# The triangular inverses of a gated delta rule: 128x128 products against 32x32 squares on the diagonal of the array, with background tasks held to one step in two ticks

## The chip, the cores and the metric

The kernel runs on one core of a Trainium2 chip. The metric is the device time of one execution in microseconds; the number to beat is the median of several runs. TensorE (PE) multiplies, VectorE (DVE) and ScalarE (ACT) do the elementwise work, GpSimd (POOL) sets up masks, and SyncE (SP) issues the transfers. Each engine works its own instructions strictly in the order in which the program hands them over, and waits where an operand is not there yet.

## The reference

A trunk of two layers on 256 tokens of width 2048, each a token mixer and an MLP of width 8192. The mixer of layer 0 is what the change touches: eight heads of a gated delta rule and eight heads of band attention behind one input projection, joined by one output projection. Per head and chunk of 64 tokens the delta rule needs the inverse of a unit lower triangular matrix:

```
lower = jnp.where(strict, jnp.einsum('bhnid,bhnjd->bhnij', kb, kc) * decay, 0.0)
tmat  = triangular_solve(eye + lower, eye)          # 64 x 64, unit lower triangular
u = tmat @ (vc * beta);   w = tmat @ (kb * exp(gcum))
# scan over the chunks:
v_new = u_n - w_n @ state
o_n   = qd_n @ state + qk_n @ v_new
state = state * gl_n + kd_n.T @ v_new
o = rms_norm(o, norm_w) * silu(z)
```

The kernel takes chunks of 128 tokens instead of 64, so its triangular matrices are 128x128, and there are two of them per head (t = 0, 1).

## The kernel before

**The big stream.** All large products are streamed: 1 MB of weights arrives in a `raw` buffer (4 of them), ACT rounds it to `wh`, DVE forms the rest `wl = raw - wh`, and PE multiplies both with activations that are split the same way. One such megabyte is an *item*. An item hands over its matmuls in four pieces, and after each piece the program makes a *tick*. At a tick the scheduler `tick` may step the task at the head of the `fast` list (evacuations of projections), steps `bg_n` background tasks (`bg_step`, round robin over `self.bg`), and pumps the modulation job: 1 MB rows (`mraw`) that DVE multiplies and sums (L466). So the order of the side work against the big stream is set by ticks, and each engine's queue is the result. Big products into `pg` belong to the input projections, those into `pw` to the output projections and later parts.

**The first mixer.** After the partial sums of the projections come, in this order, eight last parts, then blocks of four items each: attention v, two gate projections in a small item, attention q, k, v of the second head group, and `GZ`, `GZ + 1`, the gates z of delta-rule groups 0 and 1. Then the output projection `out_blocks` starts; its first two items take the units of group 0 (`o[0]`) and of attention group 0 (`o[2]`), the third takes `o[3]` and `o[1]`, and `o[1]` is delta-rule group 1. Where a unit is asked for and isn't finished, `unit_of` and `gdn_z` step its task to the end on the spot.

**The delta rule.** The background tasks are two groups of four heads (`gdn_group`; group 1 starts when group 0 is done, `gdn_after`) and two attention groups. A group runs `gdn_tile` for t = 0, 1 in lockstep: norms, decay E, values V, the matrix `lt` (transposed lower part, 128x128 for each head), `Pt` for the output. Then comes the inverse by doubling, s = 2, 4, 8, 16, 32, 64: with X the inverse of the diagonal blocks of size s, `y = mask(lt.T x)`, `x = x - xt.T y`, then `xt` is x transposed by PE and copied by ACT. Each level is 4 + 4 products of 128x128 in f32 and 4 transposes, for each t. Only the blocks on the diagonal hold anything, but the products run over the whole 128x128. Then the tail of the group, one chain: `gvn` = Xt V, `gS` = kd v, `gR`, `gvn` of t = 1, the outputs `go` through `Pt`, squares, a root by Newton's steps (`gor`, `goss`, `goy`, `gon`, `got`), the scaling, transposes into the result. `gdn_z` multiplies with the gate and splits for the output projection.

`bg_n` is 1.5 here: one and a half background steps at each tick.

Of the kernel before, what the change touches and what calls it, by code (L numbers as in the profile page):

```python
# [12 lines left out]
I32 = mybir.dt.int32  # L13
AF = mybir.ActivationFunctionType
# [4 lines left out]
P = 128  # L19
# [20 lines left out]
class Task:  # L40


    def __init__(self, gen):
        self.gen, self.done, self.result = gen, False, None
        self.n, self.frees = 0, 10000
# [67 lines left out]
class Trunk:  # L113
# [8 lines left out]
    def __init__(self, tc, ctx, ins, out):  # L122
# [15 lines left out]
        self.ticks = 0  # L138
# [74 lines left out]
    def bg_step(self):  # L213
        for _ in range(len(self.bg)):
            t = self.bg.pop(0)
            ok = t.step()
            if not t.done:
                self.bg.append(t)
            if ok:
                return True  # L220
# [190 lines left out]
    def masks(self):  # L411
# [16 lines left out]

        self.M = {}
        for s in (2, 4, 8, 16, 32, 64):  # L430
            nb = P // (2 * s)
            m = self.const([P, nb, s], f"lev{s}")
            g.memset(m, 1.0)
            g.affine_select(out=m, in_=m, compare_op=ALU.is_ge, fill=0.0, base=-s, pattern=[[-2 * s, nb], [0, s]], channel_multiplier=1)
            g.affine_select(out=m, in_=m, compare_op=ALU.is_ge, fill=0.0, base=2 * s - 1, pattern=[[2 * s, nb], [0, s]], channel_multiplier=-1)
            self.M[s] = m

        self.M1T = self.const([P, 64, 2], "lev1T")
        g.memset(self.M1T, 0.0)
        v = self.M1T[:, :, 1:2]  # L440
        g.memset(v, 1.0)
        g.affine_select(out=v, in_=v, compare_op=ALU.is_equal, fill=0.0, base=0, pattern=[[-2, 64], [0, 1]], channel_multiplier=1)
        self.M1T = self.M1T.rearrange("p b c -> p (b c)")
# [613 lines left out]
    def gdn_tile(self, hg, t, kf, qf, vf, G):  # L1057
# [54 lines left out]

        xt = self.s2(tag="gXt")
        nc.vector.tensor_tensor(xt, lt, self.row(self.M1T), op=ALU.mult)
        nc.vector.tensor_tensor(xt, self.row(self.ident), xt, op=ALU.subtract)
# [8 lines left out]
        ps = self.pm()  # L1124
        for h in range(4):
            self.tr(ps[:, h], xt[:, h])
        x = self.s2(tag="gX")
        nc.scalar.copy(x, ps)
        G["X" + str(t)] = x
        yield  # L1130


        for s in (2, 4, 8, 16, 32, 64):
            nb = P // (2 * s)
            part = lambda a, n: a.rearrange("p h (b n c) -> p h b n c", n=2, c=s)[:, :, :, n]
            ps = self.pm()
            for h in range(4):
                self.mm(ps[:, h], lt[:, h], x[:, h])
            y = self.s2(tag="gY")
            nc.gpsimd.memset(y, 0.0)  # L1140
            nc.vector.tensor_tensor(part(y, 0), part(ps, 0), self.M[s].unsqueeze(1).to_broadcast([P, 4, nb, s]), op=ALU.mult)
            yield
# [696 lines left out]
```

## Time and profile before

| | |
|---|---|
| median of 3 runs | 2692.22 us (2691.31 to 2695.09) |
| the profiled execution | 2696.17 us, its span 2694.1 us |
| mean granted TensorE clock | 0.993 |
| busy: PE, DVE, ACT, POOL | 98%, 80%, 50%, 1% of the span |
| last copy of group 1's result (L1238) | starts at 448.9 us |
| second item of the output projection | starts at 489.1 us |

PE and its weight loads (PEld) are listed apart. A row of a group gives line, engine, operation, out<-in by the program's names, shape and count, then busy time and the mean of one. In f32 each product is two records of PE, so 192 records of `gX,gLt` are 96 products. A record's time includes the way through the array; the distance from one record to the next is shorter, and it is that distance which adds up. A row of the timeline gives start, length, engine, line, operation, count, and in square brackets the idle time before it with what ended it.

### The profile page before, as it was taken

Reading aid. Unit: us, or ns where it says so; the run is one execution under the profiler, and the core shown is the slowest. Engines: PE = TensorE matmul, PEld = TensorE weight load, DVE = VectorE, ACT = ScalarE, POOL = GpSimd, SP = SyncE. Lnnn points to the kernel's source line nnn. Section 1 sums busy time; section 2 is a strip of 40 time slices with the busy share of each in tenths; the row PEclk is TensorE's granted clock in tenths of the full one; section 3 lists DMA queues with packets and bytes.
Section 4 is the critical chain, followed back from the end, with each engine's and each line's share of the span. In section 5 each row is a group of like instructions: output and inputs, shape, how many; then the busy total and the mean of one; then the engine's idle time right before and its main releaser. Section 6 shows DMA issues by size and latency. Waiting matters only on the chain.

```text
span 2694.1 us, 40013 instructions
## 1 busy us (share of the span) xinstructions
PE 2636.1 (98%) x15834; PEld 2324.7 (86%) x15834; DVE 2153.1 (80%) x3106; ACT 1347.7 (50%) x1990; POOL 24.2 (1%) x98
## 2 busy tenths in 40 slices
PE   5999999999999999999999999999999999999999
PEld 4887989888888888888888888888888888888888
DVE  7998998997888888889889876897787855555554
ACT  3445455456355354454556544665555354454452
POOL 1000000000000000000000000000000000000000
PEclk7999999999999999999999999999999999999999
DMA  9986487867899899898556665555557855555553
GB/s 351 346 327 235 173 305 273 327 239 288 313 344 327 332 330 332 334 331 307 177 190 216 230 235 203 204 188 174 201 199 286 321 194 188 188 188 188 190 194 133
DMA packets 100459, 680.08 MB, mean 252 GB/s; under 512 B 11184, under 2 KB 14512, under 8 KB 19376
## 3 DMA queue, kind: packets, MB, share of 16 engines
q1 hardware_dynamic: 95376, 669.07, 68.5%
q10 hardware_dynamic: 4896, 8.46, 1.0%
q8 instruction: 124, 2.03, 0.3%
q14 instruction: 63, 0.52, 0.1%
HBM read 675.33 MB, written 2.16 MB: 251 GB/s over the span
## 4 chain that ended last, share of the span: by engine, by line
PE 87%; DVE 7%; DMA 3%; ACT 2%; issue 1%; ACTq 0%; DVEq 0%; SPq 0%
PE pw L332 67%; PE pg L332 13%; PE pm L335 3%; PE pm L332 2%; DVE mraw L466 2%; DVE wl L346 2%; DMA mraw<-in_mod_dram 2%; PE pm L339 1%; DMA raw<-in_w_ab_dram 1%; ACT wh L342 0%; DVE u L1619 0%; DVE hf L893 0%; DVE u L896 0%; ACT pm L1075 0%; DMA sd_rowd<-sd_rows 0%
## 5 line engine op out<-in xcount | busy, mean ns | idle before, releaser
L342 ACT CAST wh<-raw 128x1024 fp32r<-128x1024 f32 x870 | 905.6, 1051 | 985.8 <-PE pw L332 697.2
L346 DVE TENSOR_TENSOR wl<-raw,wh 128x1024 fp32r<-128x1024 f32 x870 | 1053.2, 1223 | 428.3 <-ACT wh L342 426.8
L332 PE MATMUL pw<-u,wh 128*128 128x512 f32 x5584 | 1318.9, 391 | 2.9 <-DVE u L896 1.7
L332 PEld LDWEIGHTS pw<-u,wh 128*128 128x128 f32 x5584 | 1032.7, 188 | 209.9 <-issue 1.9
L332 PEld LDWEIGHTS pw<-u,wl 128*128 128x128 f32 x5584 | 702.1, 191 | 23.5 <-DVE wl L346 2.0
L332 PE MATMUL pw<-u,wl 128*128 128x256 f32 x5584 | 712.3, 283 | 2.6 <-ACT u L342 1.4
L466 DVE SCALAR_TENSOR_TENSOR mraw<-mraw,crow 128x2048 f32<-128x2048 f32 x192 | 438.9, 2288 | 20.5 <-DMA mraw<-in_mod_dram 20.3
L332 PE MATMUL pg<-wh,u 128*128 128x512 f32 x864 | 279.5, 396 | 0.0
L332 PEld LDWEIGHTS pg<-wh,u 128*128 128x128 f32 x864 | 162.0, 188 | 33.2 <-issue 0.7
L958 DVE SCALAR_TENSOR_TENSOR x<-pw,mod,x 128x256 f32<-128x256 f32 x352 | 162.0, 480 | 32.5 <-PE pw L332 29.9
L332 PE MATMUL pg<-wl,u 128*128 128x512 f32 x432 | 169.5, 392 | 0.3
L332 PE MATMUL pg<-u,wh 128*128 128x256 f32 x672 | 124.5, 285 | 0.0
L332 PEld LDWEIGHTS pg<-u,wh 128*128 128x128 f32 x672 | 105.5, 192 | 0.3
L332 PEld LDWEIGHTS pg<-wl,u 128*128 128x128 f32 x432 | 81.2, 188 | 17.9 <-DVE wl L346 1.7
L332 PE MATMUL pg<-u,wl 128*128 128x256 f32 x336 | 95.4, 284 | 0.0
L332 PE MATMUL pm<-u,wh 128*128 128x256 f32 (+1 forms) x340 | 64.0, 292 | 19.2 <-ACT wh L342 19.2
L332 PEld LDWEIGHTS pm<-u,wh 128*128 128x128 f32 x340 | 54.3, 199 | 20.3 <-ACT wh L342 20.0
L332 PEld LDWEIGHTS pg<-u,wl 128*128 128x128 f32 x336 | 64.4, 192 | 0.0
L1017 DVE SCALAR_TENSOR_TENSOR u<-pad,cst,u 128x256 f32<-128x256 f32 x144 | 60.4, 484 | 3.9 <-ACT u L1011 3.8
L1531 ACT ACTIVATE rl<-rs 128x512 f32<-128x512 f32 x64 | 40.5, 633 | 27.7 <-DVE rs L1526 25.1
L1525 ACT COPY rs<-pw 128x512 f32<-128x512 f32 x64 | 36.8, 576 | 34.5 <-PE pw L332 34.5
L895 ACT ACTIVATE u<-hf,mod 128x256 fp32r<-128x256 f32 x64 | 29.4, 502 | 49.4 <-DVE hf L893 49.4
(298 smaller groups left out, 1525.9 us busy)
## 6 DMA issues: line engine op xcount, KB each, us to landing
raw<-in_w_dram SPq DMA_DIRECT2D x256, 1024.0 KB, 5.2
mraw<-in_mod_dram SPq DMA_DIRECT2D x192, 1024.0 KB, 6.1
raw<-in_w_ab_dram SPq DMA_DIRECT2D x56, 1024.0 KB, 5.7
raw<-in_w_ssd_dram SPq DMA_DIRECT2D x48, 1024.0 KB, 4.9
raw<-in_w_sz_dram SPq DMA_DIRECT2D x32, 1024.0 KB, 4.8
raw<-in_wo_ssd_dram SPq DMA_DIRECT2D x32, 1024.0 KB, 4.9
raw<-in_wo_ab_dram SPq DMA_DIRECT2D x16, 1024.0 KB, 5.4
sE<-sd_rowd ACTq DMA_DIRECT2D x32, 256.0 KB, 4.9
```

The costliest lines, as they stand in the source:

```text
L332: return self.nc.tensor.matmul(o, a, b, start=start, stop=stop, skip_group_check=True)
L335: self.nc.tensor.matmul(o, lhsT, rhs, start=True, stop=True, skip_group_check=True)
L339: return self.nc.tensor.transpose(o, a, self.anti if flip else self.ident[:k, :k])
L342: a = self.nc.scalar.copy(hi, src)
L346: b = self.nc.vector.tensor_tensor(lo, src, hi.bitcast(F32), op=ALU.subtract)
L466: x = nc.vector.scalar_tensor_tensor(raw, raw, 1.0, self.crow, op0=ALU.mult, op1=ALU.mult, accum_out=t[:, f : f + 1])
L895: nc.scalar.activation(hi, h[:, f], AF.Identity, bias=shift[:, col])
L958: self.last = nc.vector.scalar_tensor_tensor(x[:, 2 * b + f], ps[:, f, n], g[:, 2 * cb + f : 2 * cb + f + 1], x[:, 2 * b + f], op0=ALU.mul ...
L1017: nc.vector.scalar_tensor_tensor(h, pad[:, f, 1 + q : 257 + q], w[:, q, j : j + 1], h, op0=ALU.mult, op1=ALU.add)
L1525: nc.scalar.copy(lo, ps[:, :, 1])
L1531: nc.scalar.activation(rl, lo, AF.Relu)
```

## The change

**The inverse.** `gdn_tile` ends after `Pt`; the inverse moves to a function of its own, `gdn_inverse`, that runs once per group for both t and all four heads (eight matrices). The levels s = 2 to 16 stay inside 32x32 squares on the diagonal: the four squares of a matrix lie on partitions 0, 32, 64, 96, and the product of each square is a matmul of 32 rows, 32 columns and 32 moving columns in its own corner of the array, 32 of them per product step. `x`, `xt`, `y` are 128x256 for all eight matrices together. The transposes go from PE and ACT to DVE, which transposes 32x32 squares. The 32 level is 16 + 24 such small products, and the 64 level 8 + 8 products of 64x64, written into `XT` (128x128 for each head; zeroed by POOL). The masks become 32 wide.

**The beat.** `Task` gets a time `at`, and `bg_step` passes over a task whose time has not come; a step that did something sets `at = ticks + gap`. `gap` is 2 in the first mixer and 0 elsewhere. So a background task steps at most once in two ticks, where a lone task made up to three steps in two ticks before. The flag that lets attention group 0 start (`self.prep`) is set when both tiles are through, before the inverse.

**What it does to the order.** In all excerpts pm, pg, pw are PSUM tiles, and the number behind a name is the program's running number. PE, the levels of group 1's inverse. Before, they stand between the items of attention v and of z (pg):

```order
L332 MATMUL pg_3808<-wl_4035,u_1713 128x512
L339 MATMUL pm_3712<-ident,gX_3587 128x128 x4
L335 MATMUL pm_3718<-gX_3587,gLt_3522 128x128 x4
L339 MATMUL pm_3726<-ident,gX_3594 128x128 x4
L335 MATMUL pm_3732<-gX_3594,gLt_3535 128x128 x4
L332 MATMUL pg_3808<-wh_4034,u_1713 128x512
L335 MATMUL pm_3748<-gY_3723,gXt_3527 128x128 x4
L332 MATMUL pg_3808<-wh_4034,u_1713 128x512
L332 MATMUL pg_3808<-wl_4035,u_1713 128x512
```

Now they stand between the first two items of the output projection (pw); this is the level s = 8 and the one after it, in the second of these items:

```order
L336 MATMUL pm_4808<-gX_4442,gLt_4289 32x32 x16
L336 MATMUL pm_4808<-gX_4442,gLt_4299 32x32 x16
L336 MATMUL pm_4852<-gY_4841,gXt_4441 32x32 x32
L333 MATMUL pw_5168<-u_4317,wh_4756 128x512 x4
L333 MATMUL pw_5168<-u_4318,wh_4756 128x512 x4
L336 MATMUL pm_4887<-gX_4442,gLt_4289 32x32 x16
L336 MATMUL pm_4887<-gX_4442,gLt_4299 32x32 x16
L333 MATMUL pw_5168<-u_4788,wh_4760 128x512 x4
L333 MATMUL pw_5168<-u_4789,wh_4760 128x512 x4
L333 MATMUL pw_5168<-u_4317,wl_4757 128x256
L336 MATMUL pm_4922<-gY_4920,gXt_4441 32x32 x32
```

So this part moved by some nine items down the stream. PE, the tail of group 1, before:

```order
L335 MATMUL pm_4005<-gV_3493,gXt_3527 128x128 x4
L332 MATMUL pg_4202<-u_761,wh_4194 128x256
L332 MATMUL pg_4202<-u_761,wl_4195 128x256
L332 MATMUL pg_4202<-u_761,wh_4194 128x256 x2
L332 MATMUL pg_4202<-u_761,wl_4195 128x256
L332 MATMUL pg_4202<-u_761,wh_4194 128x256 x2
L332 MATMUL pg_4202<-u_761,wl_4195 128x256
L335 MATMUL pm_4020<-gvn_4010,gkd_3316 128x128 x4
L332 MATMUL pg_4202<-u_761,wh_4194 128x256 x2
```

and now, from the 64 level on (`gX_651` is `x64`):

```order
L336 MATMUL pm_5016<-gX_651_4455,gLt_4299 64x64 x4
L336 MATMUL pm_5027<-gXT_4453,gY_5025 64x64 x4
L336 MATMUL pm_5027<-gXT_4454,gY_5025 64x64 x4
L336 MATMUL pm_5038<-gV_4226,gXT_4453 128x128 x4
L336 MATMUL pm_5045<-gvn_5043,gkd_3980 128x128 x4
L336 MATMUL pm_5052<-gS_5050,u_2425 128x128 x4
L336 MATMUL pm_5062<-gS_5050,u_2521 128x128 x4
L336 MATMUL pm_5069<-gR_5057,gXT_4454 128x128 x4
L336 MATMUL pm_5077<-gvn_5043,gPt_4347 128x128 x4
L336 MATMUL pm_5088<-gvn_5074,gPt_4354 128x128 x4
L340 MATMUL pm_5122<-ident,go_5082 128x128 x4
L340 MATMUL pm_5128<-ident,go_5093 128x128 x4
```

The big products are gone from between the links; ahead of these rows the 32 level stands likewise without them, down from the end of the second `pw` item, and the third begins behind them. DVE at the same place, before:

```order
L1180 TENSOR_TENSOR gvn_4010<-pm_4005,gbe_3415 128x512
L346 TENSOR_TENSOR wl_4264<-raw_4257,wh_4263 128x1024
L1193 SCALAR_TENSOR_TENSOR gR_4049<-pm_4044,gd_neg,gV_3500 128x128 x4
L1198 TENSOR_TENSOR gqS_4059<-pm_4054,gd_eg 128x512
L1204 TENSOR_TENSOR gvn_4074<-pm_4069,gbe_3442 128x512
L466 SCALAR_TENSOR_TENSOR mraw_4467,mod_126<-mraw_4467,crow 128x2048
L1216 TENSOR_TENSOR go_4112<-gqS_4059,pm_4107 128x512
```

and now:

```order
L478 SCALAR_TENSOR_TENSOR mraw_5310,mod_126<-mraw_5310,crow 128x2048
L1196 TENSOR_SCALAR gX_651_4455<-pm_4986 32x8x32
L486 TENSOR_TENSOR mod_126<-mod_126,cst 128x4
L1213 TENSOR_SCALAR gXT_4453<-pm_5027 64x4x64
L1213 TENSOR_SCALAR gXT_4454<-pm_5027 64x4x64
L478 SCALAR_TENSOR_TENSOR mraw_5364,mod_127<-mraw_5364,crow 128x2048
L1237 TENSOR_TENSOR gvn_5043<-pm_5038,gbe_4102 128x512
L486 TENSOR_TENSOR mod_127<-mod_127,cst 128x4
L488 SCALAR_TENSOR_TENSOR mod_127<-mod_127,cst 128x4
L1250 SCALAR_TENSOR_TENSOR gR_5057<-pm_5052,gd_neg,gV_4233 128x128 x4
L1255 TENSOR_TENSOR gqS_5067<-pm_5062,gd_eg 128x512
L1261 TENSOR_TENSOR gvn_5074<-pm_5069,gbe_4129 128x512
```

One multiplication of the modulation job (L478 there, L466 before) stands ahead of the links `gX_651` and `gvn`. SP's queue differs in one place only: two weight transfers are issued ahead of one `mraw` instead of behind it.

The diff (the masks cut short):

```diff
--- before.py
+++ after.py
@@ -42,7 +42,7 @@
 
     def __init__(self, gen):
         self.gen, self.done, self.result = gen, False, None
-        self.n, self.frees = 0, 10000
+        self.n, self.frees, self.at = 0, 10000, 0
 
     def step(self):
 
@@ -135,7 +135,7 @@
         self.fast, self.bg, self.open = [], [], []
         self.fast_n, self.bg_n = 0.5, 0.5
         self.credit = self.fcredit = 0.0
-        self.ticks = 0
+        self.ticks = self.gap = 0
         self.pending = self.early = self.etask = None
         self.pin = self.still = 0
         self.after_ins = self.gate = None
@@ -213,10 +213,11 @@
     def bg_step(self):
         for _ in range(len(self.bg)):
             t = self.bg.pop(0)
-            ok = t.step()
+            ok = t.at <= self.ticks and t.step()
             if not t.done:
                 self.bg.append(t)
             if ok:
+                t.at = self.ticks + self.gap
                 return True
         return False
 
@@ -426,21 +427,32 @@
+        def diagonal(name, full):
+
+            m = self.const([P, 32], name)
+            for b in range(4):
+                B = slice(32 * b, 32 * b + 32)
+                g.tensor_copy(m[B], full[B, B])
+            return m
+
+        self.I32 = diagonal("I32", self.ident)
         self.M = {}
-        for s in (2, 4, 8, 16, 32, 64):
+        for s in (2, 4, 8, 16):
...
+            self.M[s] = diagonal(f"lev{s}", full)
...
+        self.M1T = diagonal("lev1T", full)
@@ -1109,10 +1121,7 @@
         lt = self.s2(tag="gLt")
         for h in range(4):
             nc.vector.scalar_tensor_tensor(lt[:, h], ps[:, h], be[:, h : h + 1], E[:, h], op0=ALU.mult, op1=ALU.mult)
-
-        xt = self.s2(tag="gXt")
-        nc.vector.tensor_tensor(xt, lt, self.row(self.M1T), op=ALU.mult)
-        nc.vector.tensor_tensor(xt, self.row(self.ident), xt, op=ALU.subtract)
+        G["lt", t] = lt
         yield
         ps = self.pm()
         for h in range(4):
@@ -1121,41 +1130,89 @@
         nc.vector.tensor_tensor(p1, ps, E, op=ALU.mult)
         G["Pt", t] = p1
         yield
-        ps = self.pm()
-        for h in range(4):
-            self.tr(ps[:, h], xt[:, h])
-        x = self.s2(tag="gX")
-        nc.scalar.copy(x, ps)
-        G["X" + str(t)] = x
-        yield
-
-
-        for s in (2, 4, 8, 16, 32, 64):
-            nb = P // (2 * s)
-            part = lambda a, n: a.rearrange("p h (b n c) -> p h b n c", n=2, c=s)[:, :, :, n]
-            ps = self.pm()
-            for h in range(4):
-                self.mm(ps[:, h], lt[:, h], x[:, h])
-            y = self.s2(tag="gY")
-            nc.gpsimd.memset(y, 0.0)
-            nc.vector.tensor_tensor(part(y, 0), part(ps, 0), self.M[s].unsqueeze(1).to_broadcast([P, 4, nb, s]), op=ALU.mult)
-            yield
-            ps = self.pm()
-            if s < 64:
-                for h in range(4):
-                    self.mm(ps[:, h], xt[:, h], y[:, h])
-                nc.vector.tensor_tensor(part(x, 0), part(x, 0), part(ps, 0), op=ALU.subtract)
-                yield
-                ps = self.pm()
-                for h in range(4):
-                    self.tr(ps[:, h], x[:, h])
-                nc.scalar.copy(xt, ps)
+
+    def gdn_inverse(self, G):
+
+
+
+        nc = self.nc
+        lt = [G["lt", t] for t in range(2)]
+        heads = [(4 * t + h, t, h) for t in range(2) for h in range(4)]
+        B = [slice(32 * b, 32 * b + 32) for b in range(4)]
+        sub = [slice(4 * t, 4 * t + 4) for t in range(2)]
+        tile = lambda tag: self.s2([P, 8, 32], tag=tag)
+        flat = lambda a: a.rearrange("p n c -> p (n c)")
+        psum = lambda: self.pm([P, 512])[:, :256].rearrange("p (n c) -> p n c", c=32)
+        rep = lambda m, n: m.unsqueeze(1).to_broadcast([m.shape[0], n, 32])
+        xt, x = tile("gXt"), tile("gX")
+        for t in range(2):
+            for b in B:
+                nc.vector.tensor_tensor(xt[b, sub[t]], lt[t][b, :, b], rep(self.M1T[b], 4), op=ALU.mult)
+        nc.vector.tensor_tensor(xt, rep(self.I32, 8), xt, op=ALU.subtract)
+        nc.vector.transpose(flat(x), flat(xt))
+        XT = [self.s2(tag="gXT") for _ in range(2)]
+        x64 = self.s2([P, 8, 64], tag="gX6")
+        for z in XT:
+            nc.gpsimd.memset(z, 0.0)
+        nc.gpsimd.memset(x64[B[0], :, 32:], 0.0)
+        yield
+
+        for s in (2, 4, 8, 16):
+            ps = psum()
+            for n, t, h in heads:
+                for b in B:
+                    self.mm(ps[b, n], lt[t][b, h, b], x[b, n])
+            y = tile("gY")
+            nc.vector.tensor_tensor(y, ps, rep(self.M[s], 8), op=ALU.mult)
+            yield
+            ps = psum()
+            for n, t, h in heads:
+                for b in B:
+                    self.mm(ps[b, n], xt[b, n], y[b, n])
+            nc.vector.tensor_tensor(x, x, ps, op=ALU.subtract)
+            if s < 16:
+                nc.vector.transpose(flat(xt), flat(x))
             else:
-                for h in range(4):
-                    self.mm(ps[:, h], y[:, h], xt[:, h])
-                nc.vector.tensor_tensor(part(xt, 1), part(xt, 1), part(ps, 1), op=ALU.subtract)
-                yield
-        G["Xt", t] = xt
+                for t in range(2):
+                    for b in B:
+                        nc.vector.transpose(XT[t][b, :, b], x[b, sub[t]])
+            yield
+
+        ps = psum()
+        for n, t, h in heads:
+            for p in (0, 2):
+                self.mm(ps[B[p + 1], n], lt[t][B[p], h, B[p + 1]], x[B[p], n])
+        y = tile("gY")
+        for p in (0, 2):
+            nc.scalar.copy(y[B[p + 1]], ps[B[p + 1]])
+        nc.gpsimd.tensor_copy(x64[B[0], :, :32], x[B[0]])
+        nc.gpsimd.tensor_copy(x64[B[1], :, 32:], x[B[1]])
+        yield
+        ps = psum()
+        for n, t, h in heads:
+            self.mm(ps[B[1], n], XT[t][B[1], h, B[1]], y[B[1], n])
+            for p in (0, 2):
+                self.mm(ps[B[p], n], y[B[p + 1], n], XT[t][B[p + 1], h, B[p + 1]])
+        nc.vector.tensor_scalar(x64[B[1], :, :32], ps[B[1]], -1.0, None, op0=ALU.mult)
+        for t in range(2):
+            for p in (0, 2):
+                nc.scalar.activation(XT[t][B[p], :, B[p + 1]], ps[B[p], sub[t]], AF.Copy, scale=-1.0)
+        yield
+
+        lower, upper = slice(0, 64), slice(64, P)
+        ps = self.pm([P, 8, 64])
+        for n, t, h in heads:
+            self.mm(ps[upper, n], lt[t][lower, h, upper], x64[lower, n])
+        y = self.s2([P, 8, 64], tag="gY")
+        nc.scalar.copy(y[upper], ps[upper])
+        yield
+        ps = self.pm([P, 8, 64])
+        for n, t, h in heads:
+            self.mm(ps[lower, n], y[upper, n], XT[t][upper, h, upper])
+        for t in range(2):
+            nc.vector.tensor_scalar(XT[t][lower, :, upper], ps[lower, sub[t]], -1.0, None, op0=ALU.mult)
+            G["Xt", t] = XT[t]
+        yield
 
     def gdn_group(self, hg, kc, qc, vc, gates):
 
@@ -1169,9 +1226,9 @@
             for t in tiles:
                 if not t.done:
                     t.step()
-            if all("X" + str(n) in G for n in range(2)):
-                self.prep[hg].done = True
-            yield
+            yield
+        self.prep[hg].done = True
+        yield from self.gdn_inverse(G)
 
         ps = self.pm()
         for h in range(4):
@@ -1667,7 +1724,7 @@
                                  ((0, (2,)), (0, (3, 4)), (0, (5,)), (1, (0, 1)), (1, (2,)), (1, (3, 4)), (1, (5,))))
         self.rate, self.rate2 = 0.25, 1.1
         self.fast_n = 0.8
-        self.bg_n = 1.5
+        self.bg_n, self.gap = 1.5, 2
         o, res = [None] * 4, {}
         put = lambda key, gen: res.__setitem__(key, self.evac(gen))
         self.prep = [Flag(), Flag()]
@@ -1739,7 +1796,7 @@
                 self.c_blocks(w, (cb,), hl, lambda ps, cb: conv_sink(ps, cb, then))
 
         self.rate = 0.0
-        self.bg_n = 0.75
+        self.bg_n, self.gap = 0.75, 0
         self.fast_n = 0.5
         for half in range(2):
             G = range(half * 4, half * 4 + 4)
```

18 lines of the change are left out of this document (9 added, 9 removed).

## The prediction

> **What bounds the kernel now.** I read the page first, then busy time by stretches around the delta rule, then PE's waits there, then the timeline.
>
> ```profile
> span 2694.1 us, 40013 instructions
> PE 2636.1 (98%) x15834; PEld 2324.7 (86%) x15834; DVE 2153.1 (80%) x3106; ACT 1347.7 (50%) x1990; POOL 24.2 (1%) x98
> ```
>
> ```profile
> 260.00:340.00 80.00, 79.79 (x535) 72.09 (x534) 77.08 (x172) 37.91 (x85) 6.12 (x18) 1.00 0.49 179
> 380.00:440.00 60.00, 60.00 (x468) 56.75 (x467) 55.51 (x100) 27.37 (x63) 3.99 (x8) 1.00 0.83 305
> 465.00:560.00 95.00, 94.96 (x592) 85.55 (x591) 92.41 (x131) 49.59 (x79) 0.00 (x0) 1.00 0.89 325
> ```
>
> The columns are the stretch, its length, then PE, PEld, DVE, ACT, POOL, the granted clock and the transfers. In the first two stretches the two inverses run, in the third the output projection. PE is full in all three and DVE stands just behind it (77.08 of 80). PE's waits from 240 to 560 us come to 3.1 us, and nearly all of it is two links of chains:
>
> ```profile
> PE pm L339 <- DVE go L1230: 1.4, 2, 0.7
> PE pm L339 <- DVE aq L1283: 0.8, 1, 0.8
> ```
>
> Since a busy PE need not be at its peak, I checked by the distance between records. In the chain of work, eight f32 records of 128 columns take 0.89 us and four transposes 0.44 us, so 0.111 us each; 16 `pw` products of 512 columns start 3.70 us before what follows them, 0.231 us each.
>
> ```profile
> 281.56 0.89 PE pm L335 x8
> 282.45 0.44 PE pm L339 x4
> ```
>
> ```profile
> 489.11 3.86 PE L332 MATMUL pw<-u,wh 128*128 128x512 f32 x16
> 492.81 4.12 PE L332 MATMUL pw<-u,wl 128*128 128x256 f32 x33
> 496.76 3.59 PE L332 MATMUL pw<-u,wh 128*128 128x512 f32 x15
> ```
>
> 33 products of 256 columns take 3.95 us, 0.120 us each, so an item of 16 + 16 needs 5.6 us of PE, and products stand back to back. PE's work sets the time here: a microsecond of it saved is a microsecond gained, and a microsecond in which PE must wait with nothing to do is lost.
>
> **The change part by part: PE's work.** What goes:
>
> ```profile
> L335 PE MATMUL pm<-gX,gLt 128*128 128x128 f32 x192 | 25.2, 275 | 0.0
> L335 PE MATMUL pm<-gY,gXt 128*128 128x128 f32 x160 | 20.0, 275 | 0.0
> L339 PE MATMUL pm<-ident,gX 128*128 128x128 f32 x80 | 12.3, 273 | 0.0
> L335 PE MATMUL pm<-gXt,gY 128*128 128x128 f32 x32 | 4.1, 275 | 0.0
> L339 PE MATMUL pm<-ident,gXt 128*128 128x128 f32 x16 | 2.4, 274 | 0.0
> ```
>
> 480 records at 0.111 us are 53.3 us. What comes, per group: 4 levels of 32 + 32 products of 32 columns, 16 + 24 for the 32 level, that is 296 products or 592 records, and 16 products of 64x64. For two groups 1184 small records and 64 of 64 columns. No product of 32 columns is in the trace. The nearest is the second layer's `sx,sE`: 64 columns, two halves of the array in turn.
>
> ```profile
> 1733.74 1.11 PE L332 MATMUL pw<-u,wl 128*128 128x256 f32 x8
> 1734.79 2.09 PE L335 MATMUL pm<-sx,sE 128*64 128x64 f32 x64
> 1736.80 3.14 PE L332 MATMUL pw<-u,wl 128*128 128x256 f32 x24
> ```
>
> 64 records in 2.01 us: 0.031 us, where half of 0.111 would be 0.056; the halves overlap by a factor 1.77. For 32 columns a quarter of 0.111 is 0.028 if squares don't overlap; with the same factor it would be 0.016; and if squares pay as a 64-column record alone, 0.056. I take 0.028, since it is nearest to the one dense row of short records, 0.031. So 1184 x 0.028 = 33.2 us. The 64 records of 64x64 all lie in one quarter, so nothing overlaps: 64 x 0.056 = 3.6 us. Entering a burst: eight products at 0.120 from 1733.74 end at 1734.70, the burst starts at 1734.79, so 0.09 us; 24 bursts make 2.1. PE's work: -53.3 + 33.2 + 3.6 + 2.1 = **-14.4 us**.
>
> The Trainium skill ("TensorE: Matmul & The Clock Gate", Part 1, on the issue floor) says that starts of matmuls never come closer than about 25 ns however few columns stream. By that the 1184 records would take at least 29.6 us and the sum would be some 3.6 us lower at best; no run here shows the floor, and 0.031 does not contradict it.
>
> **DVE, ACT, POOL.** DVE loses 24 `gY` and 20 `gX` operations and what forms the first `xt`:
>
> ```profile
> L1141 DVE TENSOR_TENSOR gY<-pm,lev 128x256 f32<-128x256 f32 x24 | 9.9, 423 | 0.6 <-PE pm L335 0.6
> L1328 DVE TENSOR_SCALAR as<-as,asum 128x128 f32<-128x128 f32 x5 | 1.4, 283 | 0.0
> L1345 ACT COPY u<-pm 128x256 f32<-128x256 f32 x5 | 1.8, 368 | 7.4 <-PE pm L332 7.4
> L466 DVE SCALAR_TENSOR_TENSOR mraw<-mraw,crow 128x2048 f32<-128x2048 f32 x33 | 75.5, 2289 | 1.0 <-DMA mraw<-in_mod_dram 1.0
> ```
>
> 44 operations at 0.42 are 18.5 us. What is left per group is 9 operations and 4 transposes of 128x256 and 19 small ones of 128 to 512 elements; taking 0.42 and 0.28 to 0.35 for them (a transpose on DVE is not in the trace; from 0.28, the smaller row, to twice 0.42) that is about 11 us a group. With the forming of `xt` that goes too, DVE ends some 3 us lower; hidden behind PE either way, except in the chain below. ACT loses its 24 copies of `xt` and `x`, POOL its 24 memsets; neither bounds. The new masks on POOL (24 copies of squares) fall into the first 25 us and are first read after 260 us, so I cost them at nothing.
>
> **What the beat does to group 1.** A group is some 30 steps: 7 for the tiles, 13 for the inverse, about 10 for the tail. At one step in two ticks two groups want 120 ticks. From the start of group 0 to the output projection there are 3 last parts and 20 items of the blocks, 23 x 4 = 92 ticks. So the last 28 ticks' worth is not hidden: the levels fall beside the first two output items, 8 ticks, and what remains is stepped to the end when the third item asks for `o[1]`. That is the piece of the order without big products. In the levels the cover is 5 to 15 big products a step (0.7 to 1.9 us) against an answer of DVE of 0.42 us, behind other operations of DVE; from the order and these durations I find about 0.9 us of wait at s = 8, where two bursts follow each other, and 0.6 elsewhere: **+1.5 us**.
>
> **The bare chain.** Its second half stands in the trace of before, hidden:
>
> ```profile
> 427.27 1.13 PE L335 MATMUL pm<-gV,gXt 128*128 128x128 f32 x8
> 428.43 0.69 DVE L1180 TENSOR_TENSOR gvn<-pm,gbe 128x512 f32<-128x512 f32 x1 [0.98 <-PE pm L335]
> 429.18 1.15 PE L335 MATMUL pm<-gvn,gkd 128*128 128x128 f32 x8
> 431.01 2.05 PE L335 MATMUL pm<-gS,u 128*128 128x128 f32 x16
> 434.81 1.09 PE L335 MATMUL pm<-gvn,gPt 128*128 128x128 f32 x8
> 436.81 0.69 DVE L1216 TENSOR_TENSOR go<-gqS,pm 128x512 f32<-128x512 f32 x1
> 438.49 0.28 ACT L1218 ACTIVATE pm<-go 128x128 f32<-128x128 f32 x1
> 438.92 0.28 ACT L1218 ACTIVATE pm<-go 128x128 f32<-128x128 f32 x1
> 439.79 0.17 DVE L1224 TENSOR_TENSOR goss<-goss,gor 128x8 f32<-128x8 f32 x1 [0.37 <-ACT pm L1218]
> 439.99 0.17 DVE L1225 TENSOR_TENSOR goss<-goss,gor 128x8 f32<-128x8 f32 x1
> ```
>
> From 427.27 to the last `Pt` products' end at 435.9 it takes 8.6 us; one `mraw` (2.29) now stands ahead of `gvn`, and another ahead of `go`. I add up from the end of the s = 16 update. 32 level: products 0.9, copy of `y` by ACT 0.7 (two at up to 0.37), in their place eight transposes behind a `wl`, so 3.7 in all; 24 products 1.35; `mraw` 2.29 and the copy to `x64` 0.35, or ACT's four scalings, 1.2: to 7.0. 64 level: 0.9, 0.6 (ACT copy), 0.9, two operations 0.7, and hand-overs of 0.1 to 0.2: to 10.5. Tail to `Pt`: 8.6 and half of `mraw`, since it starts while `gV` still runs: to 20.2. `go` behind `mraw`: 22. Four squares at 0.43: 23.7. Sixteen short operations at 0.20: 26.9. Two scalings at 0.69, transposes, ACT's copies: 30. Gate and split (0.75 and 0.69 twice each, with ACT's casts): **33 us**. In it PE works on 32 + 48 short records (2.2), 32 of 64 columns (1.8), 56 of 128 (6.2) and 17 others (1.9), 12 us, all counted above. So PE stands **21 us** with nothing to do.
>
> The clock falls with it. In the second layer PE waited 2.35 us for `sE`, and:
>
> ```profile
> 1407.70 1.76 PE L335 MATMUL pm<-sx,sE 128*64 128x64 f32 x32 [2.35 <-DVE sE L1433]
> 1409.39 2.34 PE L332 MATMUL pw<-u,wh 128*128 128x512 f32 x5
> ```
>
> ```profile
> 1407.80:1408.80 1.00, 1.00 (x24) 1.00 (x26) 1.00 (x3) 0.00 (x0) 0.00 (x0) 0.60 0.96 193
> 1409.80:1410.80 1.00, 1.00 (x3) 0.75 (x3) 1.00 (x3) 0.00 (x0) 0.00 (x0) 0.50 1.07 428
> 1411.80:1412.80 1.00, 1.00 (x6) 0.84 (x5) 0.52 (x1) 0.57 (x1) 0.00 (x0) 1.00 1.02 338
> ```
>
> Granted clock 0.5 to 0.6 for some 3.6 us, and 32 records took 1.69 instead of 1.0 us. After the bare chain about 3.6 us at half speed cost 1.8, and some bursts inside run slow: **+3 us** (0 to 6). One of the waits of 3.1 us goes with the old place of the tail: **-1 us**.
>
> Sum: -14.4 + 1.5 + 21 + 3 - 1 = **+10.1 us**. The profiled execution took 2696.17 us, 4 us above the median of the runs; against the median 2692.22 I get **2702 us**.
>
> **Rivals.** *The squares overlap.* At 0.016 us (the halves' factor) PE's work falls by another 14.2 us, and with a chain that is 3 us shorter the time is 2685: faster by 0.27%. It decides from about 0.019 us a record down (there the sum is zero). For it speaks the overlap of `sx,sE`; against it that an f32 product's two records go to the same square one after the other, so only neighbours can overlap. The Trainium skill ("TensorE: Matmul & The Clock Gate", Part 3) would have different squares start about 4 ns apart, which is this rival at its strongest; its floor of Part 1 speaks against it. No run here has shown either.
>
> *The squares are dear.* At 0.056 us, if changes of shape or weight loads bar any hiding, PE's work rises by 33 us instead: 2735. Against it: the 64-column burst at 0.031 has a new weight load for each record too.
>
> *The chain is covered.* If the 33 us were 22, because ACT and DVE had nothing else queued, PE would idle 11 us less and the sum is -1: 2691, no change. Against it: the `mraw` rows in the order, and the row at 439.79.
>
> **How the numbers follow.** A time within 0.2% (5.4 us) of before can't be told from no change with runs that lie 3.8 us apart. Chances: my sum, with its 0.025 to 0.031 and a chain of 28 to 38 us, 0.57 (2695 to 2712; a fifth of it within 0.2%); overlap 0.17, two thirds of it faster by over 0.2%; covered chain 0.12, two thirds of it no change; dear squares 0.14. So faster 0.15, same 0.24, slower 0.61. The range leaves out the strongest overlap and the top of the dear squares: 2686 to 2725.
>
> **What would show it.** In the profile after: a burst of 64 small records 1.8 us long (right), 1.0 (overlap) or 3.6 (dear); PE's waits, 3.1 us before from 240 to 560, near 25 us and headed by `gvn`, `go` and `u` of group 1; a slice with a granted clock near 0.5 before the third output item. If PE's waits there stay below 10 us, the chain was covered and I am wrong on the main term.

## The result, and the profile after

The changed kernel takes 2716.4 us (median of 5 runs, 2714.2 to 2719.9) against 2694.0 of the kernel before beside it: ratio 1.0084, 95% interval 1.0073 to 1.0095. It is 22.4 us slower; 10.1 were forecast. The squares were the smaller part of the story: they turned out far cheaper than I took them, and the kernel lost all the same, because TensorE now stands idle or runs at half clock for longer than was saved.

The page of the changed kernel, and its three stretches that were shown of before:

```profile
span 2712.3 us, 41498 instructions
PE 2622.2 (97%) x16602; PEld 2299.3 (85%) x16602; DVE 2153.9 (79%) x3114; ACT 1340.3 (49%) x1980; POOL 27.9 (1%) x106
```

```profile
260.00:340.00 80.00, 70.73 (x628) 56.28 (x627) 77.74 (x176) 40.19 (x110) 2.09 (x10) 0.94 0.65 246
380.00:440.00 60.00, 57.23 (x447) 54.34 (x446) 56.63 (x120) 33.58 (x92) 1.70 (x4) 1.00 0.87 322
465.00:560.00 95.00, 76.20 (x733) 67.06 (x732) 72.30 (x130) 34.88 (x71) 1.71 (x2) 0.84 0.54 203
```

Before, PE was full in all three (79.79 of 80, 60.00 of 60, 94.96 of 95). Now it has 9 us of nothing in the first, and the granted clock falls to 0.94; DVE is as full as it was (77.74 against 77.08). In the third, where the bare chain lies, PE, DVE and the clock all fall.

All but the first six records of a burst of squares in the timeline after, with what follows them:

```profile
460.40 0.70 PE L336 MATMUL pm<-gX,gLt 32*32 32x32 f32 x58
461.04 0.94 PE L333 MATMUL pm<-aT,u 128*128 128x128 f32 x6
```

These are 58 records in 0.64 us, 0.011 us each, and 0.70 us for 64. I had set down 1.8 us for such a burst if right, 1.0 for overlap, 3.6 for dear squares. So the squares overlap more than the rival said.

PE's waits from 240 to 600 us after, the longest in total first:

```profile
PE pm L340 <- DVE go L1287: 7.0, 1, 7.0
PE pm L336 <- ACT gu L1091: 4.8, 1, 4.8
PE pg L333 <- DVE wl L347: 4.6, 4, 1.9
PE pg L333 <- ACT wh L343: 2.9, 2, 2.5
PE pm L336 <- issue: 2.6, 4, 1.2
PE pm L336 <- DVE gX L1196: 2.4, 1, 2.4
PE pm L336 <- DVE gY L1166: 2.4, 2, 1.5
PE pm L336 <- DVE gXT L1178: 2.0, 4, 1.1
PE pw L333 <- ACT u L343: 1.5, 1, 1.5
```

The bare chain stands where it was expected: `go`, `gX` (that is `x64`), `gXT`, `u`. What was not expected is that the big products themselves wait, for `wl` and `wh`, the halves of their own weights, and the wait of 4.8 us for `gu`: that one stands at 273 us, in the first steps of group 0, far ahead of the chain. The waits from 240 to 560 us come to 38.0 us, where the prediction said near 25. The chain in the timeline:

```profile
477.85 0.69 PE L336 MATMUL pm<-gX,gLt 32*32 32x32 f32 x32
484.33 1.93 PE L336 MATMUL pm<-gX,gLt 64*64 64x64 f32 x16 [2.44 <-DVE gX L1196]
489.41 2.08 PE L336 MATMUL pm<-gV,gXT 128*128 128x128 f32 x8 [0.51 <-DVE gXT L1213]
508.88 1.94 PE L340 MATMUL pm<-ident,go 128*128 128x128 f32 x8 [7.02 <-DVE go L1287]
515.18 4.00 PE L333 MATMUL pw<-u,wl 128*128 128x256 f32 x17 [1.50 <-ACT u L343]
```

```profile
490.00:495.00 5.00, 3.56 (x15) 2.97 (x14) 2.73 (x5) 0.34 (x1) 0.00 (x0) 0.50 0.37 121
```

From 477.85 to 515.18 it is 37.3 us, at a mean granted clock of 0.64: eight records of 128 columns are on PE for 2.08 us here, where they took 1.13 before.

**Where the time went.** The third output item begins at 515.2 us, before at 494.7, within the block of `wl` products that starts at 492.81: 20.5 us later. The spans of the two profiled executions lie 18.2 us apart, so the whole loss of these executions arises ahead of that item. With the measured prices PE's work there is 53.3 us less and 1184 x 0.011 + 64 x 0.067 + 2.1 = 19.4 more (0.067 is from the run with warm products below), so 33.9 less. PE must therefore stand or run slow for 54 us more. By PE's busy times about 35 of the 54 are idle time, and the other 19 are records that take longer. The chain of 37.3 us holds 11 us of work at full clock (80 records at 0.011, 32 at 0.067, 56 at 0.111, others 1.9): 26 of the 54, of which 16.4 idle. The other 28 lie ahead of it, between 240 and 478 us, where I had written +1.5.

### The profile page after: what moved, and what is told of

The parts are those of the page before. It is cut to its first block, busy times and chain, and to the rows that moved or that the text cites. A ratio compares the mean times of both kernels' runs of the same rounds, so it can differ in the third digit from the quotient of the medians.

```text
span 2712.3 us, 41498 instructions
## 1 busy us (share of the span) xinstructions
PE 2622.2 (97%) x16602; PEld 2299.3 (85%) x16602; DVE 2153.9 (79%) x3114; ACT 1340.3 (49%) x1980; POOL 27.9 (1%) x106
## 4 chain that ended last, share of the span: by engine, by line
PE 86%; DVE 10%; ACT 1%; issue 1%; DMA 1%; SPq 0%; DVEq 0%; ACTq 0%
PE pw L333 70%; PE pg L333 11%; DVE mraw L478 3%; DVE wl L347 2%; PE pm L333 2%; PE pm L336 2%; PE pm L340 1%; DVE u L1004 0%; ACT wh L343 0%; DVE u L1676 0%; DVE hf L905 0%; DMA x<-in_x_dram 0%; DVE u L908 0%; DMA sE<-sd_rowd 0%; DMA sd_rowd<-sd_rows 0%
## 5 line engine op out<-in xcount | busy, mean ns | idle before, releaser
L478 DVE SCALAR_TENSOR_TENSOR mraw<-mraw,crow 128x2048 f32<-128x2048 f32 x192 | 438.7, 2286 | 3.5 <-DMA mraw<-in_mod_dram 2.9
L1583 DVE TENSOR_TENSOR rs<-pw,rs 128x512 f32<-128x512 f32 x64 | 43.9, 686 | 9.9 <-ACT rs L1582 9.9
```

Source lines behind the costliest of these rows:

```text
L478: x = nc.vector.scalar_tensor_tensor(raw, raw, 1.0, self.crow, op0=ALU.mult, op1=ALU.mult, accum_out=t[:, f : f + 1])
L1583: nc.vector.tensor_tensor(lo, ps[:, :, 0], lo, op=ALU.add)
```

## The experiments

The kernel before was run beside each group, with medians from 2694.0 to 2695.1 us; differences below are against 2694.4, and a run is told from another by its interval.

**The inverse alone, and the beat alone.** First the changed kernel without the beat:

```diff
-        self.bg_n, self.gap = 1.5, 2
+        self.bg_n, self.gap = 1.5, 0
```

> The new inverse with the old beat (gap 0). Theory (the loss sits in group 1's chain, which the beat pushes behind the last big products, and beside it DVE bounds the stretch from 240 us on): here the order has big products between all links of the tail, so no bare chain; PE's work is 33 us lower than before, but DVE's 235 us of the 255 us from 240 us to the third output item stay, so at most 20 us can be gained: 2674 to 2685 us. Rival (the small squares themselves hold PE up, since every level waits twice for DVE, and four levels of group 1 follow each other here without a big product): 2692 to 2702 us.

Measured 2704.5 us, ratio 1.0035 (1.0022 to 1.0048). Then the old inverse with `Task.at` and a gap of 2:

```diff
-        self.bg_n = 1.5
+        self.bg_n, self.gap = 1.5, 2
```

> The old 128x128 inverse with the new beat (gap 2). Theory: the last levels and the tail of group 1 come behind the second output item here too, and PE has its old work; the bare chain costs 20 to 35 us: 2712 to 2729 us, PE's waits headed by go of group 1. Rival (the squares, not the beat, make the loss): 2688 to 2698 us.

Measured 2710.3 us, ratio 1.0056 (1.0039 to 1.0073), just under the range of the theory; PE's longest waits there are the bare chain's `go` (6.6 us) and `gu` (4.8 us, at 274 us, in the first steps of group 0), as in the changed kernel. So the beat alone costs 16 us, by the bare chain and by the steps that it shifts earlier on; no run parts the two. But my theory, that the chain is the whole loss and the inverse alone is faster, fell: the inverse alone, with no bare chain, is 10 us slower than before with 33.9 us less for PE to do. That is also above the range of the rival.

**A gap of 1.**

```diff
-        self.bg_n, self.gap = 1.5, 2
+        self.bg_n, self.gap = 1.5, 1
```

> The new inverse with gap 1, one step a tick: 60 ticks for both groups of the 92 there are, so group 1 ends beside the gate items. Theory: no bare chain, and the levels have 5 to 20 big products between them, so it comes out with or below the inverse alone: 2672 to 2683 us. Rival (squares hold PE up): 2690 us or more.

Measured 2715.6 us (1.0065 to 1.0095): the theory missed, and the number lies where the rival had it. By the code a tick makes no more steps than there are tasks, so a lone task makes one a tick in any case; a gap of 1 differs from none only where a second task stands in the list and waits. (The section on the change says that a lone task made up to three steps in two ticks; only a task with such a waiting neighbour did.) This small shift costs 11 us: two waits for the first `gX` of a group, 5.8 us at 281 us for group 0 and 7.2 at 410 for group 1, come to 13.1 us. A small change of the order costs as much here as the new inverse as a whole.

**What VectorE's queue is worth.** In the changed kernel, and after it in the kernel before and in the inverse alone, the modulation rows are multiplied over 64 of their 2048 columns, so the modulation leaves out the rest:

```diff
+                        n = 64 if self.short else 2048
-  ...scalar_tensor_tensor(raw, raw, 1.0, self.crow, ...)
+  ...scalar_tensor_tensor(raw[:, :n], raw[:, :n], 1.0, self.crow[:, :n], ...)
```

> The changed kernel, but from the last parts to the output projection the modulation rows are multiplied over 64 of their 2048 columns only (the transfers stay whole), so some 33 DVE operations of 2.29 us become short ones; the modulation is then not the reference's. Theory (between 240 and 478 us DVE is the bound, 94% busy, and PE's 36 us of idle there are waits for it): that stretch shrinks by 20 to 30 us and the chain stays: 2686 to 2698 us. Rival (PE waits there for transfers or for the short replies of the levels): less than 8 us, 2708 us or more.

> The kernel before, with the modulation rows multiplied over 64 of their 2048 columns from the last parts of the projections to the output projection (the transfers stay; the output is then another). If VectorE is only the next limit, behind a full TensorE, the old kernel gains little from it: 2686 to 2694 us, against 2694.6. If VectorE holds the old kernel as it holds the new one, it gains as much as the changed kernel did from the same edit (16 us): 2675 to 2682.

> The new inverse without the beat (2704.5 us), with the same short modulation rows. If the saved work of TensorE (33 us by the records) is lost because VectorE's rows of 2.29 us stand ahead of the levels' answers, of wl and of the raw buffers, it comes out here: 2664 to 2682. If it is lost in the order itself, levels that stand one behind another with no big product between them, whatever VectorE has in its queue, little comes back: 2692 to 2704.

| median, us | before | inverse alone | inverse and beat |
|---|---|---|---|
| full rows | 2694.4 | 2704.5 | 2716.4 |
| short rows | 2693.7 | 2687.8 | 2700.4 |
| ratio of the short one (interval) | 0.9998 (0.9988 to 1.0007) | 0.9974 (0.9963 to 0.9984) | 1.0022 (1.0012 to 1.0031) |

The old kernel came out as the first theory had it; the changed kernel 2 us above its theory's range, and the inverse alone between its two ranges. (The expectation for the changed kernel speaks of 36 us of idle time of PE from 240 to 478 us; by PE's busy time it is 21.8.) Read by columns: sparing VectorE gives the old kernel nothing, and the new inverse 16 to 17 us. Read by rows: the inverse costs 10 us with VectorE's rows and gains 6 without them, and the beat costs 12 to 13 either way. So VectorE's rows did not hold the old kernel, which fits a bound by TensorE, and they do hold the new inverse. They are not the whole of it: the inverse alone is 33.9 + 10.1 = 44 us slower than the saved work would make it, and short rows give back 16.7. The stretch from 240 to 520 us of before, of the inverse alone, and of the inverse alone with short rows:

```profile
240.00:520.00 280.00, 276.96 (x1850) 248.58 (x1849) 259.95 (x542) 149.31 (x376) 13.26 (x32) 1.00 0.70 256
```

```profile
240.00:520.00 280.00, 251.60 (x2561) 214.86 (x2561) 249.82 (x532) 137.07 (x360) 5.46 (x18) 0.91 0.65 243
```

```profile
240.00:520.00 280.00, 263.23 (x2665) 223.31 (x2666) 210.34 (x558) 141.95 (x371) 6.45 (x18) 0.97 0.69 260
```

DVE works 250 of 280 us with the new inverse, 10 less than before, so it is not full. PE stands idle for 28.4 us where it was 3.0, and the granted clock is 0.91 where it was 1.00. How DVE holds PE up is seen in the timeline of the inverse alone, where the levels of group 1 stand one behind the other:

```profile
404.96 1.99 ACT L343 CAST wh<-raw 128x1024 fp32r<-128x1024 f32 x2 [13.53 <-DMA raw<-in_w_ab_dram]
...
407.99 0.38 DVE L1166 TENSOR_TENSOR gY<-pm,lev 128x256 f32<-128x256 f32 x1
408.30 2.34 DVE L347 TENSOR_TENSOR wl<-raw,wh 128x1024 fp32r<-128x1024 f32 x2
408.43 0.75 PE L336 MATMUL pm<-gY,gXt 32*32 32x32 f32 x64 [1.13 <-DVE gY L1166]
410.56 0.41 DVE L1172 TENSOR_TENSOR gX<-gX,pm 128x256 f32<-128x256 f32 x1
410.89 2.29 DVE L478 SCALAR_TENSOR_TENSOR mraw<-mraw,crow 128x2048 f32<-128x2048 f32 x1
411.02 0.58 PE L336 MATMUL pm<-gX,gLt 32*32 32x32 f32 x25 [1.84 <-DVE gX L1172]
...
413.10 0.44 DVE L1174 STREAM_TRANSPOSE gXt<-gX 128x256 f32<-128x256 f32 x1
...
413.90 1.07 PE L336 MATMUL pm<-gY,gXt 32*32 32x32 f32 x64 [1.29 <-DVE gY L1166]
```

Each answer takes 0.4 us and stands behind a row of 2.29 us or two `wl`, 2.34 us together. From 405.8 to 423.1 us PE does nothing but seven such bursts. The weights are late as well: rows and weights share four buffers, and ScalarE waited 13.5 us for one to be loaded. (With short rows one such wait is 13.4 us too, so the time of the rows on VectorE does not explain it.) Two of PE's waits show it from the other side:

```profile
PE pg L333 <- ACT wh L343: 8.5, 1, 8.5
PE pg L333 <- DVE wl L347: 5.7, 3, 3.4
```

These two are 14.2 of the 28.4 us of idle time. What was PE's work before is now PE's waiting, in good part for these two queues, and slow records after the waits.

**Is TensorE's time worth anything there?** The inverse alone, with idle products on the identity put ahead of its bursts: 42 ahead of group 1's levels, and then 144 ahead of all bursts of both groups.

```diff
+    def warm(self, on, o, n):
+        for _ in range(n if on else 0):
+            self.mm(o[:, :P], self.ident, self.ident)
...
             ps = psum()
+            self.warm(True, flat(ps), 6)
```

> The new inverse without the beat, with 6 idle products on the identity ahead of each burst of group 1's levels from s = 4 to the first of the 32 level: 42 products, 9.3 us at full clock. If the levels' waits of 1.1 to 1.8 us let the clock fall (0.66 to 0.76 in the slices from 360 to 440) and the products behind them run at half speed, the idle work gives back 2 to 8 us: 2696 to 2702. If the clock is not worth anything there, the idle products cost nothing or some of their 9 us: 2704 to 2712.

> The new inverse without the beat, with 6 idle products ahead of every burst of both groups' inverses: 144 products, 32 us of TensorE's work at full clock, as much as the change saved. If TensorE is no longer what sets the time there, most of it disappears in the waits: 2700 to 2714. If TensorE's work still sets the time, all of it comes on top: 2728 to 2737.

The 42 gave 2708.8 us (1.0028 to 1.0061), not told apart from 2704.5; so nothing shows of a gain by the clock. But they raised it only in part, from 0.91 to 0.95 between 240 and 520 us. The 144 gave 2702.4 us (1.0016 to 1.0035), not told apart either, though 32 us of work came back. Its stretch, and the two waits from 240 to 600 us that still come to more than 2 us:

```profile
240.00:520.00 280.00, 272.37 (x2866) 238.30 (x2866) 252.58 (x537) 138.30 (x362) 7.51 (x18) 1.00 0.66 245
```

```profile
PE pm L336 <- issue: 2.4, 3, 1.5
PE pm L345 <- DVE rsy L288: 2.2, 1, 2.2
```

PE is nearly full again, at full clock, and without the waits for `wh` and `wl`; the time is the same. All that the change saved on TensorE could be put back at no cost. Two reserves: the added products also moved some big ones between the levels, and they keep the clock at 1.00, where it was 0.91. So this run changes order and clock as well as work, and what it shows is that the saved time had turned into waits and slow records, not which of the two.

**The clock in the bare chain.** The changed kernel, with 59 idle products in the waits of group 1's chain:

```diff
         ps = self.pm()
+        self.warm(hg == 1, ps[:, 0], 4)
         for h in range(4):
             self.mm(ps[:, h], G["Xt", 0][:, h], G["V", 0][:, h])
```

> The changed kernel, with 59 idle products of 128x128 on the identity (13 us of TensorE's work at full clock) put into the waits of group 1's bare chain, ahead of its bursts. If the clock of 0.5 in the chain is what stretches its bursts (11 us of work at full clock) and the first output products behind it, it gets shorter by 5 to 9 us: 2707 to 2711. If the chain's length is answers of VectorE and ScalarE alone, nothing is gained, or up to 4 us lost where an idle product stands in the way: 2715 to 2720.

Measured 2713.0 us (1.0050 to 1.0080), 3.4 less than 2716.4 and between what the two theories said; the intervals overlap, so the gain is likely and not certain. The trace is plainer:

```profile
481.06 0.69 PE L336 MATMUL pm<-gX,gLt 32*32 32x32 f32 x32 [0.84 <-DVE gX L1177]
...
487.73 1.14 PE L336 MATMUL pm<-gX,gLt 64*64 64x64 f32 x16
488.80 1.16 PE L336 MATMUL pm<-ident 128*128 128x128 f32 x8
...
491.73 1.06 PE L336 MATMUL pm<-gV,gXT 128*128 128x128 f32 x8
...
513.15 2.29 PE L333 MATMUL pw<-u,wl 128*128 128x256 f32 x17 [1.50 <-ACT u L348]
```

```profile
490.00:495.00 5.00, 4.22 (x42) 3.97 (x43) 3.79 (x7) 0.00 (x0) 0.00 (x0) 1.00 0.24 100
```

The clock is 1.00 throughout the chain, eight records take 1.06 instead of 2.08 us, and the chain is 32.1 us long instead of 37.3. The 17 `wl` products behind it take 2.1 us from start to start of the next group, instead of 3.8. The chain began 3.2 us later than in the changed kernel, which takes back nearly half of that. What is left of the chain beside 11 us of work, 21 us, is answers of DVE and ACT.

**Three other orders.** Modulation at an even pace, rows shared with GpSimd, fewer steps a tick, each on the inverse alone:

```diff
-        self.rate, self.rate2 = 0.25, 1.1
+        self.rate, self.rate2 = 0.58, 0.58
...
-        self.rate = 0.5
+        self.rate = 0.58
```

> The new inverse without the beat, with the modulation rows paced evenly (0.58 a tick from the last parts to the output projection, in place of 0.25, 1.1 and 0.5). If weights come late because rows of the dense stretch hold the raw buffers until VectorE gets to them (ScalarE waits 13.5, 4.3 and 4.3 us for raw there), an even pace gives back 6 to 16 us: 2688 to 2699. If VectorE's sum of work is the limit, whenever it is done, nothing changes: 2701 to 2708.

Measured 2711.0 us (1.0046 to 1.0076), worse than both theories said.

```diff
+                        if self.share and f % 2:
+                            nc.gpsimd.tensor_tensor(raw, raw, self.crow, op=ALU.mult)
+                            x = nc.scalar.activation(raw, raw, AF.Copy, accum_out=t[:, f : f + 1])
...
```

> The new inverse without the beat (2704.5 us), with every second modulation row of the first mixer multiplied by GpSimd in place and summed by ScalarE, so that VectorE is spared about half of its 2.29 us rows there; the result is the full one. Half of what the short rows gave (16.7 us) would be 8: 2692 to 2699. The rival: GpSimd's product over 2048 columns, which no trace shows, is so slow that it holds the raw buffers longer than VectorE did and weights come later: 2704 to 2720.

Measured 2774.8 us (1.0277 to 1.0308): the rival was right, and by more than it said. Two groups of its trace and its longest wait of PE:

```profile
L480 POOL TENSOR_TENSOR mraw<-mraw,crow 128x2048 f32<-128x2048 f32 x17 | 82.1, 4832 | 139.6 <-DMA mraw<-in_mod_dram 71.7 <-DVE mraw L483 23.8 <-DVE am L1386 21.8
L483 DVE SCALAR_TENSOR_TENSOR mraw<-mraw,crow 128x2048 f32<-128x2048 f32 x18 | 45.1, 2509 | 0.0
```

```profile
PE pg L334 <- DVE wl L348: 16.5, 5, 9.4
```

GpSimd takes 4.83 us where DVE takes 2.29, and DVE's own rows, 2.29 us before, take 2.51 beside it. That the buffers are held longer fits the wait for `wl`; how much of the loss each part makes, the run does not show.

```diff
-        self.bg_n, self.gap = 1.5, 2
+        self.bg_n, self.gap = 1.1, 0
```

> The new inverse without the beat, with 1.1 background steps a tick in place of 1.5, so that group 1 ends just before the output projection. By the order, 7 to 16 big products then stand between any two bursts of group 1's levels, where none stood from s = 4 on with 1.5. If the saved work is lost because the levels' waits have no cover in the order, TensorE's idle time goes down with the waits, and a good part of the 33 us comes out: 2672 to 2692. If VectorE's sum of work between 240 and 520 us holds the kernel in any order, it stays where the inverse alone was: 2698 to 2708.

Measured 2714.4 us (1.0064 to 1.0092): a miss on both sides. The levels had their cover, and what waits is spread over more than a dozen links, headed by `gu` (4.8 us), attention's `as` (4.7) and `gV` (4.7). No order that was tried makes the new inverse faster than the kernel before.

**What stays open.** With short rows the inverse alone gains 6 of 33.9 us, and there neither PE (263 of 280) nor DVE (210) is full. The trace shows waits of PE of 16.9 us from 240 to 520 us, over ten links, and a clock of 0.97; which of them could be taken out, and whether by order alone, no run settles. One of them no theory above had. It stands among the small squares and has no releaser in the profile ("issue"), and its two longest cases split a burst in two:

```profile
PE pm L337 <- issue: 7.4, 5, 2.5
```

```profile
372.42 0.54 PE L337 MATMUL pm<-gY,gXt 32*32 32x32 f32 x38
375.43 0.43 PE L337 MATMUL pm<-gY,gXt 32*32 32x32 f32 x26 [2.47 <-issue]
...
384.26 0.38 PE L337 MATMUL pm<-gY,gXt 32*32 32x32 f32 x23
387.00 0.79 PE L337 MATMUL pm<-gY,gXt 32*32 32x32 f32 x41 [2.35 <-issue]
```

The operands were there, since the first records of the burst read the same tiles, and behind each of the two stops the granted clock is 0.50. In each stop the trace has one transfer of the queue that loads instructions. Whether PE waits there for its own instructions (a burst is 64 records and as many weight loads in 0.7 us) was not tried. The kernel before has no such wait between 240 and 520 us, the inverse alone 1.2 us and the changed kernel 2.6.

The kernel takes its steps in ticks, but the order in each queue is made when the program is built, by a scheduler with estimates of its own: the seven bursts without big products between them belong to seven different ticks. The front of this document tells only of the ticks. Whether that scheduler's estimate of a square is at fault was not tried.

## Why the prediction was right or wrong

The time lay in the range of 2686 to 2725 us and on the side that was forecast, and 22.4 us were lost where 10.1 were said; it is above the 2695 to 2712 that the sum itself was given. That it came so near is in part luck: PE's work fell by 19.5 us more than the sum had it, and the waits and slow records ahead of the chain took 26.5 us more, so two large errors in good part cancel. By its own steps:

- *PE's work, -14.4.* The term was mis-sized: the 1184 small records cost 0.011 us each instead of 0.028, 13.0 us instead of 33.2; the 64 records of 64x64 cost 0.067 instead of 0.056. The sum was -33.9 us. The nearest row, `sx,sE` with two halves in turn, did not carry over to four squares; the argument against overlap (two records of a product in the same square) did not hold.
- *"A microsecond of it saved is a microsecond gained."* This is the step that failed. It was read from a full PE in the old kernel, and there it fits that sparing VectorE gave nothing; how many microseconds of saving it would have held for, no run shows. In the row it was read from, DVE stood at 77.08 of 80. In the new inverse it does not hold: 33.9 us less work made the kernel 10 us slower, and 144 idle products put on top cost nothing. What was saved on TensorE came back as its waits and as records at half clock. VectorE's rows make 16.7 of these 44 us; the cause of the rest stays open.
- *The levels, +1.5.* The whole stretch from 240 to 478 us took about +28. I counted waits of the level's own links, 0.6 to 0.9 us each, and held everything else to be covered; I did not ask whether weights could come faster than before.
- *The bare chain, 33 us long with 21 idle, and the clock, +3.* Right in place and length: 37.3 us with 26 idle or slow, against 24 for the two terms together, and 32.1 us where idle products kept the clock at 1.00. The clock was mis-sized: it makes 5 us within the chain and 1.7 on the first products behind it. Of the three links that were to head the waits `go` did (7.0 us), while `u` (1.5) and `gvn` (1.1) came far down. The change minus the inverse alone, 11.9 us, is less than the 26; that VectorE meanwhile does work which would have held PE up elsewhere would explain it, but no run shows it.
- *The rivals.* Overlap was right about the squares, with a price (0.016) still above the 0.011 measured, and wrong about the time (2685), since it used the step that failed. Dear squares and the covered chain were wrong. The chance of 0.61 for slower rested on the chain, and the chain came.
- *The Trainium skill* ("TensorE: Matmul & The Clock Gate", Part 1, on the issue floor) was named with starts of matmuls no closer than about 25 ns. The trace disagrees: 11 ns a record over bursts of 58 to 64. Part 3 of that page, with starts on different squares some 4 ns apart, is nearer.

## What to carry to other kernels

Before a saving on the bounding engine is counted as time, ask what that engine will wait for once the work is gone: the second engine in the same stretch (DVE stood at 92 to 97% behind a full PE here), the order of its own queue, and the clock that falls in the waits. Of 33.9 us of saved products nothing came out here, and 6 us with VectorE's rows cut short. Two runs help to find out cheaply: shorten the second engine's largest operation in both kernels, and put idle work back on the first. They tell how much hangs on the second engine and whether the saved time is used at all; what makes up the rest has to be looked for in the trace. And when side work is thinned out, see who asks for its result last: what is not done by then is stepped to the end with no cover, and here it ran at a mean clock of 0.64 on top.

## What the runs showed of the hardware

- In a burst that goes round the four diagonal squares, a record of an f32 product of 32x32x32 costs 11 ns (58 records in 0.64 us), where a record of 128 columns over the whole array takes 111 ns (eight in 0.89 us).
- DVE's transpose of 32x32 squares over 128x256 f32 takes 0.44 us, and 0.41 to 0.42 us is what it takes to subtract over as much.
- In the chain of the changed kernel the granted clock falls to 0.50 at 482 us, after a stretch of 4 us in which PE was busy for 1.89 us, between waits of 0.24 to 1.05 us; with 4 to 9 idle products of 128x128 ahead of six of its bursts, and 28 ahead of that on `go`, it stays at 1.00. The Trainium skill ("TensorE: Matmul & The Clock Gate", Part 1, "What's actually happening") has the clock fall to half after an idle window of some 3.4 us; the trace agrees with the half, and shows it with no single wait that long ahead of it.
- GpSimd multiplies 128x2048 f32 by another tile in 4.83 us against 2.29 on DVE, which also sums them: a factor of 2.1. The Trainium skill ("GPSIMD Engine Reference", 4.1) says about twice as slow for two inputs, and the trace agrees. DVE's rows beside it grow by a tenth, from 2.29 to 2.51 us.
- A burst of 32x32 records can stop in its midst for 2.35 to 2.47 us with nothing in the profile that released it (the inverse alone with short rows, 372 and 384 us).
